# Gelu by ScalarE's own function, a 512-column u pass, half as many compressed-score products, and norm weights folded into w_out, in a one-core hybrid decoder block

## The chip, the cores and the metric

The kernel runs on one core of a Trainium2 chip. The metric is the device time of one execution in microseconds (us). A profile of one execution lies beside it: what each engine did and what it waited for. The engines are TensorE (PE; its weight loads are listed apart as PEld), VectorE (DVE), ScalarE (ACT), GpSimd (POOL) and SyncE (SP), which issues all the transfers.

## The reference, cut to what matters

One layer of a decoder block on 512 tokens of width 1024. One input projection gives u and v (512 columns each), q (512), the keys and values (768) and 24 gate logits. Group A is a spatial gate: gelu(u) times a causal mix of layer_norm(gelu(v)). Group B is sparse attention with three branches; the compressed branch scores each query against 31 compressed keys:

```
a = spatial_gating_unit(gelu(u), gelu(v), ...)
s_cmp = einsum('bthgd,bnhd->bhgtn', q, kc) * scale
p_cmp = masked_softmax(s_cmp, cmp_end[None, :] <= t_pos[:, None])
b = gated sum of the compressed, selected and window branches
mixed = concatenate([rms_norm(a, mix_out_g[0]), rms_norm(b, mix_out_g[1])])
x = x + mixed @ w_out
x = x + memory_cross_attention(rms_norm(x), mem, ...)
x = x + square(relu(rms_norm(x) @ w_ff1)) @ w_ff2
```

gelu is the tanh form, 0.5 z (1 + tanh(0.798 (z + 0.0447 z^3))).

## The kernel before, in words

Every float32 operand of a product is split in two: a rounded high part (`hi`) and the rest (`lo`). `mm3` makes one product of three: hi by hi, hi by lo, lo by hi. A weight block comes in by `granule`: one transfer into `raw`, then `hi` as a copy (on ACT or DVE, whichever the planner finds sooner) and `lo` as a subtraction on DVE.

The program text doesn't issue anything by itself. It records operations in a `Plan`, and `Plan.schedule` sets the order: it walks through time with a cost for each operation, and among the operations that could start first on an engine it takes the one with the highest rank. The rank is the operation's place in the text, moved by the number that the table `LEADS` holds for its stage (`u0`, `ln`, `pc13`, `wo_b1`, ...). The engines then run their instructions strictly in that order. All instructions therefore bear the line of `issue` (L393 to L397), and groups are told apart by tiles: `ps` is a PSUM bank, `w` and `raw` weight blocks, `b` a large buffer, `z`, `q` and `P` work tiles of 512 columns.

The stages that the change touches:

- The v and u projections (`proj`), recorded as fill work beside the attention: v as one pass of 512 columns, u as two passes of 256 (`u0`, `u256`). ACT moves each result out of PSUM with the scale `rx`. Then `gelu2` makes gelu of two ACT functions (Square, Tanh) and two DVE operations per tile of 512 columns, and gives 2 gelu(z); the norms after it put the factor right with 4 EPS.
- `cprep`, once for each of 4 token blocks and 2 key heads: for each of 4 heads one product of the queries `qT` (128 columns of weights) with the high and one with the low part of the compressed keys `KC`, 32 columns each, into one bank on top of the mask `cmk` (a product with the identity). DVE takes the maximum and subtracts it, ACT takes Exp, DVE sums, divides and gates, and PE transposes the tile `pc`.
- `evac`, which collects the attention's output in `bT`; for a finished token block it takes the mean square and multiplies `bT` by the norm weights `gmx[:, 1]` on DVE. `wo_b` splits `bT` and multiplies with the second half of w_out.

The attention's scores, softmax (Exp on ACT, tile `P`), scaling (DVE or POOL), transposes and value products run through all of this.

Of the kernel before, what the change touches and what calls it, by code (L numbers as in the profile page):

```python
# [10 lines left out]
F32R = mybir.dt.float32r  # L11
# [44 lines left out]

LEADS = {"ch_f0": -786, "ch_f1": -935, "ch_norm0": -3881, "ch_norm1": -4239, "ch_norm3": -5516, "ch_o0": 272,
# [20 lines left out]


class Plan:  # L80
# [14 lines left out]
    WARM = 6400  # L95

    SPARE = (0, 300, 0, 0, 0)

    def __init__(self, tc, share):
        self.tc, self.nc, self.share = tc, tc.nc, share  # L100
        self.ops, self.loads, self.lead, self.queue, self.stage, self.stages = [], [], 0.0, None, None, []
        self.home, self.last, self.reads = {}, {}, {}
        self.tiles, self.uses, self.caps, self.index = [], [], {}, {}
        for e in self.ENGINES:
            setattr(self, e, self._Engine(self, e))
# [31 lines left out]
    def cost(self, eng, op, aps, func):  # L137
# [5 lines left out]
        if eng == "sync":  # L143
            run = min(list(a.ap)[-1][1] for a, _ in aps)
            return max(450, 4 * n * max(list(a.ap)[0][1] for a, _ in aps) / (260 if run <= 128 else 360))
        psum = any(bank for _, bank in aps)
# [15 lines left out]
    def locks(self, eng, op, reads, writes):  # L162

        if eng == "gpsimd":
            return op not in ("memset", "affine_select")
        if eng != "vector":
            return False
        inner = [a for a in reads if self.width(a) > 1 and not self.in_bank(a)]
        if op == "square":
            return len(inner) == 1  # L170
        if op in ("tensor_copy", "tensor_scalar"):
            return self.width(writes[0]) > 16 and len(inner) == 1
        return op in ("tensor_tensor", "scalar_tensor_tensor") and len(inner) > 1
# [27 lines left out]
    def add(self, ways, args, kw):  # L201
# [7 lines left out]
        for group, write in ((reads, False), (writes, True)):  # L209
            for a in group:  # L210
# [41 lines left out]
                for e, op in ways]  # L252
        self.loads.append(self.load(ways[0][1], args[1]) if ways[0][0] == 0 else 0.0)
        self.stages.append(self.stage)
        self.ops.append((ways, args, kw, sorted(deps), used, self.lead + LEADS.get(self.stage, 0) - i))

    def schedule(self):
# [13 lines left out]
        ends = [{} for _ in self.tiles]  # L271
        free, begun = [0.0] * ne, 0.0

# [26 lines left out]
        def start(i, e):  # L300
            t = max(free[e], begun + self.loads[i]) if e == 0 else free[e]
            if e in port and next(w for w in ops[i][0] if w[0] == e)[3]:
                t = max(t, port[4 - e])
            for x in range(ne):
                t = max(t, known[i][x] + lat[x][e])
            return t
# [31 lines left out]
        while len(out) < len(ops):  # L338
# [26 lines left out]
            if e == 0:  # L365
                begun = t
            span = max(span, end)
            if shared:
# [32 lines left out]
def hybrid_block(ctx, tc, x, mem, norm_mix_g, w_in, sg_ln_g, sg_ln_b, sg_w, sg_b, q_norm_g,  # L401
# [92 lines left out]

    def granule(src, keep=False, before=None):

# [13 lines left out]
        if before:  # L510
            for i in range(a):
                before(i)
                c = slice(i * b, i * b + b)
                dma(raw[:, c], src[:, i, :])
                split_any(raw[:, c], hi[:, c], lo[:, c])
        else:
            dma(raw.rearrange("p (a b) -> p a b", a=a), src)
            split_any(raw, hi, lo)
        hi, lo = (v.rearrange("p (a b) -> p a b", a=a) for v in (hi, lo))
        return [(hi[:, i, :], lo[:, i, :]) for i in range(a)]  # L520

    def grans(w, k0, nk, c0, ncol):
        v = w.rearrange("(k p) n -> p k n", p=P)
        step = min(nk, 1024 // ncol)
        r = []
        stage = nc.stage
        for k in range(k0, k0 + nk, step):
            nc.stage = f"{stage}.w{c0}.{k}"
            r += granule(v[:, k:k + step, c0:c0 + ncol])
        nc.stage = stage  # L530
        return r
# [124 lines left out]
    VBv = VB.rearrange("p (b h t) d -> p b h t d", b=2, h=NKV)  # L656
    KC = cpool.tile([P, 2, NKV, 32], F32R, name="KC")
    gates = cpool.tile([P, TT, 24], F32, name="gates")
# [193 lines left out]
    for i in range(2):  # L852
        nc.tensor.transpose(tp[:, i * HD:i * HD + HD].bitcast(F32R), kch[:, i].rearrange("p s d -> p (s d)"),
                            idr[:HD, :HD])
    nc.scalar.copy(KC, tp.rearrange("p (i h n) -> p i h n", i=2, h=NKV))

# [9 lines left out]
    vz = b8([P, TT, SG], F32)  # L866
    ps = proj(512, 512)
    for t in range(TT):
        act(vz[:, t, :], ps[t], AF.Copy, scale=rx[:, t:t + 1])
    nc.stage = "ln"  # L870
    gelu2([(vz[:, t, :], ztile()) for t in range(TT)])
    mvs, rvs = [], []
    for t in range(TT):
# [3 lines left out]
        mvs.append(mv)  # L877
        rvs.append(rsqrt(mv[:, 1:2], 1.0, 4.0 * EPS))
    for t in range(TT):
# [3 lines left out]
        split(w, vbh[:, t, :], vbl[:, t, :])  # L883
    for c in (0, 256):
        nc.stage = f"u{c}"
        ps = proj(c, 256)
        nc.stage = f"gu{c}"
        for t in range(TT):
            act(u2[:, t, c:c + 256], ps[t][:, :256], AF.Copy, scale=rx[:, t:t + 1])
        gelu2([(u2[:, t:t + 2, c:c + 256], ztile().rearrange("p (t c) -> p t c", t=2)) for t in (0, 2)])  # L890

# [24 lines left out]
    def cprep(t, kvh, qT):  # L916

        ps = bank()[:, :G * 32].rearrange("p (g n) -> p g n", g=G)
        nc.tensor.matmul(ps, idb, bc(cmk[:, t, None, :], [P, G, 32]), start=True, stop=False)
        for g in range(G):  # L920
            for i in range(2):
                nc.tensor.matmul(ps[:, g, :], qT[:, g * P:g * P + P], KC[:, i, kvh, :], start=False,
                                 stop=g == G - 1 and i == 1)
        mx, den, c = small(G), small(G), small(G)
        dve.tensor_reduce(mx, ps, AX.X, OP.max)
        e = zpool.tile([P, G, 32], F32, tag="pc", bufs=2, name=nm("pc"))
        dve.tensor_tensor(e, ps, bc(mx[:, :, None], [P, G, 32]), OP.subtract)
        act(e, e, AF.Exp)
        dve.tensor_reduce(den, e, AX.X, OP.add)
        dve.reciprocal(c, den)  # L930
        g3 = gates[:, t, :].rearrange("p (h b) -> p h b", b=3)
        dve.tensor_tensor(c, c, g3[:, kvh * G:kvh * G + G, 0], OP.mult)
# [8 lines left out]
    class Pair:  # L941
# [79 lines left out]
        def evac(self):  # L1021
# [12 lines left out]
            if kb == 3:  # L1034
# [3 lines left out]
                rb[t] = rsqrt(stats(ps, SG), 1.0 / SG, EPS)  # L1038
                dve.tensor_tensor(bT[t], bT[t], bc(gmx[:, 1, :, None], [P, 4, P]), OP.mult)

# [76 lines left out]
    for t in range(TT):  # L1117
        ra.append(rsqrt(stats(u2[:, t, :], SG), 1.0 / SG, 4.0 * EPS))

# [64 lines left out]
    def wo_b(t):  # L1184
        if not wso:
            wso.extend(p for blk in range(2) for p in grans(w_out2, 4, 4, blk * 512, 512))
        bh, bl = qpair()
# [238 lines left out]
```

## Time and profile before

| | us |
|---|---|
| median of 3 runs | 705.9 |
| the 3 runs | 703.88, 707.63, 705.9 |
| the profiled execution, its time | 703.69 |
| its span, first to last instruction | 701.8 |

The span is what the trace shows; 1.9 us of the profiled execution's time lie outside it. Busy time of an engine is the time in which at least one of its instructions ran; a product's own duration is longer than the distance to the next one, since products overlap, so costs of products are read from start to start.

### The profile page before, as it was taken

How to read it: one execution, taken by the hardware profiler on the slowest of the kernel's cores; microseconds unless marked ns; L12 is line 12 of the kernel's file. 1: busy time of each engine (PE TensorE's matmuls, PEld its weight loads, DVE VectorE, ACT ScalarE, POOL GpSimd, SP SyncE). 2: the span in 40 equal slices, each digit the busy share in tenths (PEclk: the TensorE clock that was granted, in tenths of full speed). 3: DMA queues.
4: the chain of work that ended last, by engine and by line, in shares of the span. 5: the costliest groups of instructions: out<-in, count | busy, mean ns of one | idle time of the engine just before them, and what ended most of it. 6: DMA issues, size and time to landing. Idle time of an engine off the chain costs nothing.

```text
span 701.8 us, 9905 instructions
## 1 busy us (share of the span) xinstructions
PE 694.0 (99%) x3768; PEld 588.2 (84%) x3768; DVE 424.4 (60%) x794; ACT 316.6 (45%) x643; POOL 78.8 (11%) x118
## 2 busy tenths in 40 slices
PE   8999999999999999999999999999999999999997
PEld 7898879988888889889888888888888888888886
DVE  6596899998899898679844223332225344433433
ACT  6454467877778776476434124332123122111210
POOL 1002112141330421133000000000000000000000
PEclk9999999999999999999999999999999999999999
DMA  9633543445222000414143332333213322223203
GB/s 291 173 101 98 189 126 122 146 136 163 61 91 98 24 1 1 150 32 120 32 118 93 96 111 83 99 99 111 91 61 121 116 94 90 91 101 109 91 0 121
DMA packets 64702, 71.05 MB, mean 101 GB/s; under 512 B 3160, under 2 KB 48976, under 8 KB 64656
## 3 DMA queue, kind: packets, MB, share of 16 engines
q1 hardware_dynamic: 64656, 70.42, 32.2%
q8 instruction: 30, 0.49, 0.3%
q14 instruction: 16, 0.13, 0.1%
HBM read 68.32 MB, written 2.10 MB: 100 GB/s over the span
## 4 chain that ended last, share of the span: by engine, by line
PE 94%; DMA 2%; DVE 2%; ACT 1%; issue 1%; SPq 0%; DVEq 0%; ACTq 0%
PE ps L397 94%; DMA raw<-in_w_in_dram 1%; DVE w L397 1%; DMA raw<-in_cmp_w_dram 1%; DMA b<-in_x_dram 1%; DVE b L397 1%; DVE z L397 0%; ACT w L397 0%; ACT b L397 0%; DVE s L397 0%; SPq L397 0%; ACT z L397 0%; ACT q L397 0%; DVEq L1421 0%; ACTq L397 0%
## 5 line engine op out<-in xcount | busy, mean ns | idle before, releaser
L397 PE MATMUL ps<-w,q 128*128 128x512 f32 x960 | 225.4, 391 | 0.0
L397 PEld LDWEIGHTS ps<-w,q 128*128 128x128 f32 x960 | 178.5, 188 | 36.0
L397 ACT CAST w<-raw 128x1024 fp32r<-128x1024 f32 (+2 forms) x95 | 97.8, 1034 | 237.4 <-PE ps L397 221.4
L397 DVE TENSOR_TENSOR w<-raw,w 128x1024 fp32r<-128x1024 f32 (+2 forms) x117 | 137.8, 1181 | 96.9 <-ACT w L397 96.2
L397 PE MATMUL ps<-w,b 128*128 128x512 f32 (+3 forms) x928 | 187.0, 355 | 1.1 <-DVE w L397 0.8
L397 PEld LDWEIGHTS ps<-w,b 128*128 128x128 f32 (+1 forms) x928 | 149.4, 187 | 24.3 <-DVE w L397 1.9
L397 PE MATMUL ps<-b,w 128*128 128x512 f32 x720 | 164.6, 389 | 0.0
L397 PEld LDWEIGHTS ps<-b,w 128*128 128x128 f32 x720 | 134.8, 188 | 27.7
L397 DVE TENSOR_TENSOR b<-ps,b 128x512 fp32r<-128x512 f32 (+2 forms) x88 | 54.3, 635 | 12.4 <-ACT b L397 8.9
L397 PE MATMUL ps<-b,b 128*128 128x256 f32 (+1 forms) x344 | 57.3, 294 | 0.0
L397 ACT CAST b<-ps 128x512 fp32r<-128x512 f32 (+1 forms) x84 | 44.5, 551 | 21.3 <-PE ps L397 20.4
L397 DVE CAST q<-b 128x512 fp32r<-128x512 f32 x24 | 10.3, 427 | 70.2 <-PE ps L397 70.2
L397 PEld LDWEIGHTS ps<-b,b 128*128 128x128 f32 x344 | 48.2, 192 | 1.5 <-ACT b L397 0.4
L397 POOL TENSOR_SCALAR P<-P,s,gates 128x128 f32<-128x128 f32 (+3 forms) x53 | 33.5, 643 | 92.9 <-DVE s L397 58.7
L397 PE MATMUL ps<-idf,P 128*128 128x128 f32 x192 | 38.3, 280 | 0.0
L397 ACT ACTIVATE P<-ps,s 128x128 f32<-128x128 f32 (+3 forms) x64 | 33.7, 533 | 7.0 <-DVE s L397 6.7
L397 DVE TENSOR_REDUCE s<-ps 128x2 f32<-128x512 f32 (+4 forms) x64 | 35.3, 564 | 2.5 <-PE ps L397 2.1
L397 ACT ACTIVATE z<-ps 128x512 f32<-128x512 f32 (+3 forms) x43 | 23.0, 581 | 27.7 <-PE ps L397 27.7
L397 DVE CAST w<-raw 128x1024 fp32r<-128x1024 f32 (+2 forms) x22 | 13.8, 631 | 31.3 <-PE ps L397 30.6
L397 POOL TENSOR_TENSOR r<-s,negh 128x1 f32<-128x1 f32 (+2 forms) x25 | 20.3, 815 | 98.0 <-DVE s L397 97.9
L397 PE MATMUL ps<-b,q 128*128 128x256 f32 (+2 forms) x96 | 27.5, 347 | 0.5 <-ACT q L397 0.5
L397 PEld LDWEIGHTS ps<-idf,P 128*128 128x128 f32 x192 | 24.2, 141 | 1.2 <-POOL P L397 0.4
(156 smaller groups left out, 576.7 us busy)
## 6 DMA issues: line engine op xcount, KB each, us to landing
raw<-in_w_ff_dram SPq DMA_DIRECT2D x64, 512.0 KB, 4.0
raw<-in_w_in_dram SPq DMA_DIRECT2D x12, 512.0 KB, 3.9
raw<-in_cmp_w_dram SPq DMA_DIRECT2D x8, 512.0 KB, 4.2
raw<-in_w_out_dram SPq DMA_DIRECT2D x8, 512.0 KB, 3.9
raw<-in_w_mkv_dram SPq DMA_DIRECT2D x8, 512.0 KB, 3.8
b<-in_x_dram SPq DMA_DIRECT2D x8, 256.0 KB, 4.9
raw<-in_w_in_dram SPq DMA_DIRECT2D x8, 256.0 KB, 5.2
b<-in_x_dram SPq DMA_DIRECT2D x4, 512.0 KB, 4.2
```

The lines of the kernel that those rows point to most:

```text
L397: getattr(getattr(self.nc, eng), op)(*a, **k)
```

## The change

`gelu2` stays for the small compression network alone. For u and v ACT now applies `Gelu_apprx_tanh` while it moves the result out of PSUM: one instruction per tile, with the same scale. It gives gelu itself, so the norms use EPS. The planner learns that this function and Exp/Tanh belong to different tables and that a change of table costs ACT a load (1283 in `TABLE`). u is projected in one pass of 512 columns. `KC` holds high and low part of a head side by side, so `cprep` makes one product of 64 columns per head; DVE adds mask and halves. The multiplication of `bT` by the norm weights goes; the second half of w_out is split with a scale instead (`gain`). The planner's transfer costs, its rule on when GpSimd holds the port that it shares, and the whole table `LEADS` are new, so every engine's order is new.

```
-LEADS = {"ch_f0": -786, "ch_f1": -935, ...
+LEADS = {"ch_f0": -1174, "ch_f1": -1572, ...
...
+    TABLES, TABLE = {AF.Exp: 0, AF.Tanh: 0, AF.Gelu_apprx_tanh: 1}, 1283
...
-            return max(450, 4 * n * max(list(a.ap)[0][1] for a, _ in aps) / (260 if run <= 128 else 360))
+            return max(450, 4 * n * max(list(a.ap)[0][1] for a, _ in aps) / (230 if run <= 128 else 290))
...
-            return op not in ("memset", "affine_select")
+            return op != "dma_start"
...
+            if e == 2 and self.tables[i] not in (None, table):
+                t += self.TABLE
...
-            split_any(raw, hi, lo)
+            for i in range(a if gain is not None else 0):
+                c = slice(i * b, i * b + b)
+                split(raw[:, c], hi[:, c], lo[:, c], scale=gain[:, i:i + 1])
+            if gain is None:
+                split_any(raw, hi, lo)
...
-    KC = cpool.tile([P, 2, NKV, 32], F32R, name="KC")
+    KC = cpool.tile([P, NKV, 2, 32], F32R, name="KC")
...
-        act(vz[:, t, :], ps[t], AF.Copy, scale=rx[:, t:t + 1])
+        act(vz[:, t, :], ps[t], AF.Gelu_apprx_tanh, scale=rx[:, t:t + 1])
     nc.stage = "ln"
-    gelu2([(vz[:, t, :], ztile()) for t in range(TT)])
...
-    for c in (0, 256):
-        nc.stage = f"u{c}"
-        ps = proj(c, 256)
-        nc.stage = f"gu{c}"
-        for t in range(TT):
-            act(u2[:, t, c:c + 256], ps[t][:, :256], AF.Copy, scale=rx[:, t:t + 1])
-        gelu2([(u2[:, t:t + 2, c:c + 256], ztile().rearrange("p (t c) -> p t c", t=2)) for t in (0, 2)])
+    nc.stage = "u"
+    ps = proj(0, SG)
+    nc.stage = "gu"
+    for t in range(TT):
+        act(u2[:, t, :], ps[t], AF.Gelu_apprx_tanh, scale=rx[:, t:t + 1])
...
-        nc.tensor.matmul(ps, idb, bc(cmk[:, t, None, :], [P, G, 32]), start=True, stop=False)
         for g in range(G):
-            for i in range(2):
-                nc.tensor.matmul(ps[:, g, :], qT[:, g * P:g * P + P], KC[:, i, kvh, :], start=False,
-                                 stop=g == G - 1 and i == 1)
+            nc.tensor.matmul(ps[:, g], qT[:, g * P:g * P + P], KC[:, kvh], start=True, stop=True)
...
-        dve.tensor_reduce(mx, ps, AX.X, OP.max)
-        dve.tensor_tensor(e, ps, bc(mx[:, :, None], [P, G, 32]), OP.subtract)
+        dve.tensor_tensor(e, ps[:, :, 1, :], bc(cmk[:, t, None, :], [P, G, 32]), OP.add)
+        dve.tensor_tensor(e, ps[:, :, 0, :], e, OP.add)
+        dve.tensor_reduce(mx, e, AX.X, OP.max)
+        dve.tensor_tensor(e, e, bc(mx[:, :, None], [P, G, 32]), OP.subtract)
...
-                dve.tensor_tensor(bT[t], bT[t], bc(gmx[:, 1, :, None], [P, 4, P]), OP.mult)
...
-            wso.extend(p for blk in range(2) for p in grans(w_out2, 4, 4, blk * 512, 512))
+            wso.extend(p for blk in range(2) for p in grans(w_out2, 4, 4, blk * 512, 512, gain=gmx[:, 1]))
```

The order of PE before, at the first compressed scores (`ps_303`): mask, then eight products with `KC`, among the attention's first scores (`KL`, `tri`) and the first u pass (`w_275`).

```order
L397 MATMUL ps_298<-b_9_89,q_290 128x256
L397 LDWEIGHTS idb
L397 MATMUL ps_303<-cmk,idb 128x128
L397 MATMUL ps_303<-KC,q_290 128x32 x8
L397 MATMUL ps_298<-KL,q_290 128x256
```

The same scores (`ps_291`) in the changed kernel: their four products stand in turn with transposes of the mixing matrix `wg`, behind products of the u pass of 512 columns (`ps_266`, `ps_267`). The first of them:

```order
L405 MATMUL ps_266<-w_275,b_8_86 128x512
L405 MATMUL ps_266<-w_277,b_6_84 128x512
L405 MATMUL ps_267<-w_275,b_6_84 128x512
L405 MATMUL ps_291<-KC,q_278 128x64
L405 MATMUL ps_689<-idf,wg 128x128
```

The scores' tile `pc_295` comes back to PE as a transpose; the four rows ahead of it and itself:

```order
L405 MATMUL ps_267<-w_277,b_6_84 128x512 x2
L405 MATMUL ps_267<-w_277,b_8_86 128x512
L405 MATMUL ps_267<-w_277,b_6_84 128x512 x2
L405 MATMUL ps_267<-w_277,b_8_86 128x512
L405 MATMUL ps_296<-idf,pc_295 128x128
```

From the last product with `KC` to this transpose stand one transpose of `wg` and 40 products of 512 columns of the u pass, and nothing else. The mask's product is gone, and there are four products with `KC` where eight stood.

The order of ACT before, at the end of v's gelu: Square and Tanh of `b_139` through the tiles `z`, then the attention's first Exps (`P`), with no load of a table.

```order
L397 ACTIVATE b_139_233<-ps_237,rx 128x512
L397 CAST q_290<-ps_291 128x512
L397 ACTIVATE z_249<-b_139_233 128x512
L397 ACTIVATE z_248<-z_248 128x512
L397 CAST w_287<-raw_286 128x1024
L397 ACTIVATE z_249<-z_249 128x512
L397 ACTIVATE P_295,s_294<-ps_292,s_293 128x128
L397 ACTIVATE P_296,s_294<-ps_292,s_293 128x128
```

The same place in the changed kernel, from the copy of `KC` that PE's four products wait for to the Exp of `pc_295`: two loads of a table stand in the queue, one ahead of three Gelus (v's third and fourth tile, u's first), one ahead of the Exps.

```order
L405 CAST KC<-ps_228 128x2x2x32
L405 CAST b_136_230<-z_262 128x512
L405 ACT_TABLE_LOAD
L405 ACTIVATE b_139_233<-ps_236,rx 128x512
L405 ACTIVATE b_139_233<-ps_237,rx 128x512
L405 ACTIVATE b_138_232<-ps_266,rx 128x512
L405 CAST b_136_230<-z_263 128x512
L405 ACT_TABLE_LOAD
L405 ACTIVATE P_289,s_288<-ps_286,s_287 128x128
L405 ACTIVATE P_290,s_288<-ps_286,s_287 128x128
L405 ACTIVATE pc_295<-pc_295 128x128
```

Over the whole program ACT has one load of a table before and seven after: three times to Gelu's table and back, all around the v and u passes.

## Rows read from the trace of the kernel before

**Rows 1.** The page, busy time by engine: us, share of span, instructions.
```profile
PE 694.0 (99%) x3768; PEld 588.2 (84%) x3768; DVE 424.4 (60%) x794; ACT 316.6 (45%) x643; POOL 78.8 (11%) x118
```

**Rows 2.** Chain of work that ended last, in order of time: start, us, what.
```profile
81.26 5.79 DMA raw<-in_w_in_dram
...
95.41 34.39 PE ps L397 x267
...
133.06 88.46 PE ps L397 x557
...
221.65 476.44 PE ps L397 x2401
```

**Rows 3.** Waits of PE over the whole span: us in total, times, longest.
```profile
PE ps L397 <- DVE zero L397: 1.1, 1, 1.1
PE ps L397 <- DMA b<-in_x_dram: 0.9, 1, 0.9
PE ps L397 <- DVE w L397: 0.8, 1, 0.8
PE ps L397 <- ACT q L397: 0.5, 1, 0.5
PE ps L397 <- DVE z L397: 0.4, 1, 0.4
```

**Rows 4.** Timeline of PE around the first compressed scores: start, us, instructions merged.
```profile
110.36 0.23 PE L397 MATMUL ps<-cmk,idb 128*128 128x128 bf16 x1
110.40 1.04 PE L397 MATMUL ps<-KC,q 128*128 128x32 f32 x8
111.30 0.36 PE L397 MATMUL ps<-KL,q 128*128 128x256 f32 x1
...
111.54 17.52 PE L397 MATMUL ps<-w,b 128*128 128x256 f32 x144
128.90 0.88 PE L397 MATMUL ps<-b,b 128*128 128x256 f32 x6
```

**Rows 5.** Timeline of PE in the second feed-forward product, a long unbroken run.
```profile
525.17 155.00 PE L397 MATMUL ps<-w,q 128*128 128x512 f32 x683
```

**Rows 6.** Busy time in one window: PE, PEld, DVE, ACT, POOL; clock, DMA share, GB/s.
```profile
100.00:140.00 40.00, 39.47 (x318) 37.84 (x317) 38.21 (x81) 32.46 (x83) 7.32 (x13) 1.00 0.36 120
```

**Rows 7.** Groups of ACT's instructions by shape: busy us, mean ns | idle before.
```profile
L397 ACT ACTIVATE b<-ps,rx 128x512 f32<-128x512 f32 x12 | 8.0, 685 | 7.9 <-PE ps L397 7.9
...
L397 ACT ACTIVATE P<-ps,s 128x128 f32<-128x128 f32 x16 | 5.8, 364 | 4.2 <-DVE s L397 4.1
...
L397 ACT ACTIVATE z<-b 128x512 f32<-128x512 f32 x8 | 5.1, 634 | 0.1
L397 ACT ACTIVATE z<-z 128x512 f32<-128x512 f32 x8 | 5.0, 628 | 0.7 <-DVE z L397 0.7
L397 ACT ACTIVATE b<-ps,rx 128x256 f32<-128x256 f32 x8 | 3.6, 477 | 1.6 <-PE ps L397 1.6
...
L397 ACT ACTIVATE pc<-pc 128x128 f32<-128x128 f32 x8 | 2.5, 316 | 1.8 <-DVE pc L397 1.7
...
L397 ACT ACT_TABLE_LOAD x1 | 1.3, 1283 | 0.8 <-PEq L1412 0.8
```

**Rows 8.** Groups of DVE's instructions by shape, the same columns.
```profile
L397 DVE TENSOR_TENSOR w<-raw,w 128x1024 fp32r<-128x1024 f32 x106 | 129.6, 1225 | 91.9 <-ACT w L397 91.3
...
L397 DVE SCALAR_TENSOR_TENSOR b<-z,b 128x512 f32<-128x512 f32 x8 | 5.5, 689 | 0.4 <-ACT z L397 0.3
...
L397 DVE SCALAR_TENSOR_TENSOR z<-z,b 128x512 f32<-128x512 f32 x8 | 5.5, 688 | 0.6 <-ACT z L397 0.5
...
L397 DVE SCALAR_TENSOR_TENSOR b<-ps,cols,b 128x512 fp32r<-128x512 f32 x4 | 3.0, 748 | 0.1
...
L397 DVE TENSOR_TENSOR bT<-bT,cols 128x512 f32<-128x512 f32 x4 | 2.7, 684 | 0.0
...
L397 DVE TENSOR_TENSOR pc<-ps,s 128x128 f32<-128x128 f32 x8 | 2.3, 286 | 0.1
```

More of the change, by code (lines that the diff above doesn't have):

```diff
@@ L55 @@
          "wf": dict(w=1, raw=1)}
-LEADS = {"ch_f0": -786, "ch_f1": -935, "ch_norm0": -3881, "ch_norm1": -4239, "ch_norm3": -5516, "ch_o0": 272,
[20 rows of a table removed]
+LEADS = {"ch_f0": -1174, "ch_f1": -1572, "ch_f2": -903, "ch_norm1": 1885, "ch_norm2": 867, "ch_norm3": -7928,
[21 rows of a table added]
 class Plan:
@@ L101, in __init__ @@
         self.ops, self.loads, self.lead, self.queue, self.stage, self.stages = [], [], 0.0, None, None, []
-        self.home, self.last, self.reads = {}, {}, {}
+        self.home, self.last, self.reads, self.tables = {}, {}, {}, []
         self.tiles, self.uses, self.caps, self.index = [], [], {}, {}
@@ L253, in add @@
         self.loads.append(self.load(ways[0][1], args[1]) if ways[0][0] == 0 else 0.0)
+        self.tables.append(next((self.TABLES[a] for a in args if isinstance(a, AF) and a in self.TABLES), None))
         self.stages.append(self.stage)
@@ L271, in schedule @@
         ends = [{} for _ in self.tiles]
-        free, begun = [0.0] * ne, 0.0
+        free, begun, table = [0.0] * ne, 0.0, 0
         port = {1: 0.0, 3: 0.0}
@@ L366, in schedule @@
                 begun = t
+            if e == 2 and self.tables[i] is not None:
+                table = self.tables[i]
             span = max(span, end)
@@ L493, in rsqrt, with granule @@
         return r
-    def granule(src, keep=False, before=None):
+    def granule(src, keep=False, before=None, gain=None):
         a, b = src.shape[1:]
@@ L517, in granule, with grans @@
             dma(raw.rearrange("p (a b) -> p a b", a=a), src)
-            split_any(raw, hi, lo)
+            for i in range(a if gain is not None else 0):
[3 more added lines that the diff above has]
+                split_any(raw, hi, lo)
         hi, lo = (v.rearrange("p (a b) -> p a b", a=a) for v in (hi, lo))
         return [(hi[:, i, :], lo[:, i, :]) for i in range(a)]
-    def grans(w, k0, nk, c0, ncol):
+    def grans(w, k0, nk, c0, ncol, gain=None):
         v = w.rearrange("(k p) n -> p k n", p=P)
@@ L528, in grans @@
             nc.stage = f"{stage}.w{c0}.{k}"
-            r += granule(v[:, k:k + step, c0:c0 + ncol])
+            r += granule(v[:, k:k + step, c0:c0 + ncol], gain=gain if gain is None else gain[:, k - k0:k - k0 + step])
         nc.stage = stage
@@ L854, in hybrid_block @@
                             idr[:HD, :HD])
-    nc.scalar.copy(KC, tp.rearrange("p (i h n) -> p i h n", i=2, h=NKV))
+    nc.scalar.copy(KC.rearrange("p h i n -> p i h n"), tp.rearrange("p (i h n) -> p i h n", i=2, h=NKV))
     nc.queue, wqueue[0], nc.stage = "fill", "wf", "v"
@@ L867, in hybrid_block @@
     ps = proj(512, 512)
+    nc.stage = "gv"
     for t in range(TT):
-        act(vz[:, t, :], ps[t], AF.Copy, scale=rx[:, t:t + 1])
+        act(vz[:, t, :], ps[t], AF.Gelu_apprx_tanh, scale=rx[:, t:t + 1])
     nc.stage = "ln"
-    gelu2([(vz[:, t, :], ztile()) for t in range(TT)])
     mvs, rvs = [], []
@@ L877, in hybrid_block @@
         mvs.append(mv)
-        rvs.append(rsqrt(mv[:, 1:2], 1.0, 4.0 * EPS))
+        rvs.append(rsqrt(mv[:, 1:2], 1.0, EPS))
     for t in range(TT):
@@ L916, in cprep @@
     def cprep(t, kvh, qT):
-        ps = bank()[:, :G * 32].rearrange("p (g n) -> p g n", g=G)
-        nc.tensor.matmul(ps, idb, bc(cmk[:, t, None, :], [P, G, 32]), start=True, stop=False)
+        ps = bank()[:, :2 * G * 32].rearrange("p (g i n) -> p g i n", g=G, i=2)
         for g in range(G):
-            for i in range(2):
-                nc.tensor.matmul(ps[:, g, :], qT[:, g * P:g * P + P], KC[:, i, kvh, :], start=False,
-                                 stop=g == G - 1 and i == 1)
+            nc.tensor.matmul(ps[:, g], qT[:, g * P:g * P + P], KC[:, kvh], start=True, stop=True)
         mx, den, c = small(G), small(G), small(G)
-        dve.tensor_reduce(mx, ps, AX.X, OP.max)
         e = zpool.tile([P, G, 32], F32, tag="pc", bufs=2, name=nm("pc"))
-        dve.tensor_tensor(e, ps, bc(mx[:, :, None], [P, G, 32]), OP.subtract)
+        dve.tensor_tensor(e, ps[:, :, 1, :], bc(cmk[:, t, None, :], [P, G, 32]), OP.add)
+        dve.tensor_tensor(e, ps[:, :, 0, :], e, OP.add)
+        dve.tensor_reduce(mx, e, AX.X, OP.max)
+        dve.tensor_tensor(e, e, bc(mx[:, :, None], [P, G, 32]), OP.subtract)
         act(e, e, AF.Exp)
         dve.tensor_reduce(den, e, AX.X, OP.add)
+        g3 = gates[:, t, :].rearrange("p (h b) -> p h b", b=3)
         dve.reciprocal(c, den)
-        g3 = gates[:, t, :].rearrange("p (h b) -> p h b", b=3)
         dve.tensor_tensor(c, c, g3[:, kvh * G:kvh * G + G, 0], OP.mult)
@@ L1117, in hybrid_block @@
     for t in range(TT):
-        ra.append(rsqrt(stats(u2[:, t, :], SG), 1.0 / SG, 4.0 * EPS))
+        ra.append(rsqrt(stats(u2[:, t, :], SG), 1.0 / SG, EPS))
     nc.lead, nc.stage = 1000, "outa"
```

41 rows, old and new, of the table LEADS are left out of this document.

## The prediction

> **What bounds the kernel now.** I read the busy time of the page first: PE works 694.0 of 701.8 us [rows 1]. Then the chain that ended last: from 95.4 us to the end it is PE's own products, but for one detour of 3.3 us that ends at 133.06 [rows 2]; ahead of 95 us it runs for a while over transfers and weight splits, such as the 5.79 us of an input weight. Then PE's waits: after its start (1.1 for the first operand, 0.9 for x) they are 0.8, 0.5 and 0.4 us, 1.7 in all [rows 3]. So the time is the length of PE's stream. Work that other engines save gives at most these 1.7 us; a product taken out of PE's stream gives its whole distance; and an engine that becomes late can cost without any such bound. Busy time doesn't tell the distance between products, since they overlap: that has to be read from starts.
>
> **The change part by part.**
>
> *u in one pass.* The run of 256-column products that starts at 111.54 and holds 144 of them is followed at 128.90: 17.36 us / 144 = 0.1206 us each [rows 4]. Products of 512 columns follow each other at 155.0 / 683 = 0.227 us [rows 5]. u takes 8 blocks of its inner dimension x 4 token blocks x 3 products: before 2 x 96 = 192 of 256 columns, 192 x 0.1206 = 23.2 us; after 96 of 512, 96 x 0.227 = 21.8 us. Gain 1.4 us. It is small because a 256-column product costs little more than half of a 512-column one. The other side of the bound: if the 512-column products ran as those of the 256-column run per column, 96 x 0.241, the gain would be nothing.
>
> *Compressed scores.* Eight products of 32 columns start at 110.40 and the next instruction at 111.30: 0.90 / 8 = 0.1125 us each, nearly as long as a product of 256 columns (0.1206) in the same rows [rows 4]. So what they cost is not their columns, and 64 columns lie between two widths with almost one price: I take 0.1125 (0.1206 at most). 64 products become 32: 32 x 0.1125 = 3.6 us (3.3 at 0.1206). The mask's product goes 8 times; from its start to the next is 0.04 us [rows 4], so 0.3 us. Where the new products stand in turn with transposes the distance may be another; I found no reason for a sign.
>
> PE's stream is shorter by 1.4 + 3.6 + 0.3 = 5.3 us.
>
> *Gelu.* DVE loses 16 operations of 0.69 us on 512 columns, 11.0 us [rows 8]. ACT loses 8 Squares of 0.634 and 8 Tanhs of 0.628, 10.1 us, and 8 evacuations of 0.477 become 4 of 0.685, 1.1 us [rows 7]. I take a Gelu to last as long as the scaled evacuation that it replaces, 0.685: the Tanh of the same width (0.628) is no longer than the Square (0.634), so the function does not seem to matter. Against that stand six loads of a table; the one load of the trace took 1.283 us [rows 7], 7.7 us for six. ACT comes out 3.5 us shorter. These things happen about 100 to 140 us, where DVE is busy 38.2 of 40 us and ACT 32.5, so that ACT had 7.5 us to spare there [rows 6]. None of it is on PE's path by itself; the gain is bounded by the waits, 1.7 us, and the harm by what the loads hold up.
>
> *What the loads hold up.* ACT's queue is in order, so everything behind a load waits. I worked it through for the tightest loop that the order shows, the second pair of loads. From the copy of KC on, ACT has two copies and three Gelus of at most 0.685 (3.4), two loads (2.6), two Exps of 0.364 and the Exp of pc, 0.316 [rows 7]: 7.0 us. DVE then sums, divides, gates and scales: four operations of at most 0.286 [rows 8], 1.1 us, so pc is ready some 8.2 us after the copy. PE goes in that time through the four products with KC and four transposes (8 x some 0.11, 0.9 us) and 40 products of 0.227 (9.1 us): 10.0 us before it asks for pc. That leaves 1.8 us, or 0.9 us for each load beyond its 1.283. So I cost the loads at nothing; their cover is the u pass itself, which stands as 40 products ahead of the transpose. If the cover went, the whole 7.7 us would be in the open.
>
> The Trainium skill says more of this: ScalarE: Activation LUTs, What ACT_TABLE_LOAD costs, gives about 1283 ns for the load and about 1380 ns for a drain, 2.66 us for every switch, and its rules advise batching by table set, which three round trips do not. The load of this trace agrees with 1283; no instruction here stands close enough behind it to show the drain. By the page's figure this pair would take 2.8 us more, 1.0 beyond the slack, and an estimate over the three pairs is at most 3 us, a time of 703.6.
>
> *Scores on DVE.* cprep gets two more operations on 128 columns, 8 x 2 x 0.286 = 4.6 us [rows 8], spread over the whole attention. DVE's total gain stays: 11.0 - 4.6 = 6.4. Behind the extra 0.57 us per call stands the Exp of pc; the slack above still covers it, since ACT comes to that Exp 6.7 us after the copy.
>
> *Norm weights.* Four multiplications of bT of 0.684 leave DVE [rows 8]. Four splits of 1.225 on DVE become eight of 0.748, 1.1 us more, so DVE gains 1.6 us; ACT takes eight scaled copies of at most 0.685, 5.5 us, for four that either engine made. All of it is preparation of weights that PE uses after fill work. I take nothing, between -0.5 and +1 us.
>
> *The new order.* The transfers, the table of leads and the planner's costs change every queue. u's four transfers hold the same bytes in half as many rows. The places with waits before, ahead of 95 us, hang on transfers [rows 2]; the order can remove 1.7 us or add as much. I take nothing.
>
> **Sum.** The profiled execution took 703.69 us, near the low end of the runs shown; 703.7 - 5.3 = 698.4. On the median of 705.9 that is 700.6, and that is the forecast: **700.5 us**.
>
> **Rivals.**
> 1. *The relief counts too.* DVE is at 96% in the window of 100 to 140 us [rows 6] and loses 11 us there; the waits of 1.7 us go as well, and the short detour of the chain at 130 us. 700.6 - 1.7 = 698.9, with the low side of the unknowns some 697. Against it: only 0.5 us of the waits is in that window.
> 2. *Part of it is eaten.* A new order opens waits elsewhere, for a transfer or a late split, of 2 to 9 us, or the loads are as long as the page says: 702.5 to 709. PE is so full that any engine's lateness shows, which speaks for it; that ACT and DVE have less to do speaks against.
> 3. *Slower.* The six loads stand in the open: each holds up the Exps behind it, the tiles P come late, their transposes stop PE, and since the attention hands work on from pair to pair nothing is won back. At 1.283 us that is 7.7 - 5.3 = +2.4, 708.3, still within half a per cent. It becomes slower than that bound when each load costs more than (5.3 + 3.5) / 6 = 1.47 us in the open. At twice the row's 1.283 it gives 15.4 - 5.3 = +10.1, 716. For it: the queue is in order and Exps do stand behind each load. Against it: the slack of 1.8 us counted above.
> 4. *The shorter products don't get shorter in sum*: a 64-column product costs twice a 32-column one. Then only 1.4 + 0.3 is left, 704.2. The rows for 32 and 256 columns speak against it; I count it within rival 2.
>
> **How the numbers follow.** Half a per cent, 3.5 us, is about what a measurement of this kernel tells from no change, so faster means under 702.4 and slower over 709.4. The forecast alone, 698.9 to 702.4: 0.53. Rival 1: 0.14. Rivals 2 and 4: 0.21. Rival 3 beyond its point: 0.12. Faster 0.67, same 0.21, slower 0.12. The range leaves out rival 3 and the end of rival 2, and below reaches under rival 1 by the 2 us in which the runs shown differ from their median: 694.5 to 706.
>
> **What would show it.** Right: the runs of u at 96 products of 0.227; products with KC at about 0.11 from start to start, 32 of them; PE's busy time near 689; six loads between 95 and 140 us, each near 1.28, and no wait of PE on P, pc, q or b of over 1 us there; DVE's busy share in that window far down. Wrong: PE idle in the window of the loads, released by ACT; gaps on ACT behind each load; waits on w or raw in the first 100 us that are longer than before; or a span over 704 with PE's waits unchanged, which would mean that the distances between products in the new order are longer than those read here.

## The result and the profile after

The changed kernel takes 699.98 us (median of 5 runs) against 705.58 for the kernel before in the same comparison: a ratio of 0.9926, interval 0.9901 to 0.9952. That is 5.6 us less, faster by 0.7%; forecast were 700.5. The profiled execution took 699.56 us, with a span of 697.8; that is 4.0 us less than the span of 701.8 before, whose execution was near the low end of its runs.

The busy line of the page after, to be read against [rows 1]:

```profile
PE 689.5 (99%) x3632; PEld 579.0 (83%) x3632; DVE 415.2 (59%) x791; ACT 318.2 (46%) x634; POOL 79.2 (11%) x120
```

PE's busy time fell by 4.5 us. DVE lost 9.2 us (the prediction's terms make 11.0 - 4.6 + 1.6 = 8.0), and ACT gained 1.6 (-3.5 for the Gelus and loads, up to +5.5 for the scaled splits): near what was counted.

PE's waits after, for [rows 3]:

```profile
PE ps L405 <- DMA b<-in_x_dram: 1.1, 1, 1.1
PE ps L405 <- DVE zero L405: 1.1, 1, 1.1
PE ps L405 <- ACT z L405: 0.7, 1, 0.7
PE ps L405 <- DVE w L405: 0.7, 2, 0.5
PE ps L405 <- DVE b L405: 0.4, 1, 0.4
PE ps L405 <- ACT q L405: 0.2, 1, 0.2
```

Behind the two of the start, the small waits are 2.0 us. Before they were 1.9: to the 1.7 of [rows 3] comes one that it doesn't show:

```profile
PE ps L397 <- ACT w L397: 0.2, 1, 0.2
```

New are 0.7 us for ACT's `z` at 521 us and 0.4 for DVE's `b` at 135 us; those of DVE's `z` and of ACT's `w` went, that of ACT's `q` shrank. So the gain did not come from waits; the stream itself is shorter.

PE around the first compressed scores, for [rows 4]: start, us, instructions merged.

```profile
102.23 7.54 PE L405 MATMUL ps<-w,b 128*128 128x512 f32 x32
109.70 0.25 PE L405 MATMUL ps<-idr,z 64*128 64x64 f32 x1
...
111.58 0.19 PE L405 MATMUL ps<-KC,q 128*128 128x64 f32 x1
111.61 0.30 PE L405 MATMUL ps<-idf,wg 128*128 128x128 f32 x1
111.67 0.28 PE L405 MATMUL ps<-KC,q 128*128 128x64 f32 x1
...
112.26 9.38 PE L405 MATMUL ps<-w,b 128*128 128x512 f32 x40
121.47 0.27 PE L405 MATMUL ps<-idf,pc 128*128 128x128 f32 x1
```

Four products with `KC` and four transposes go from 111.58 to 112.26, 0.68 us in turn. The u products follow each other at 9.21 / 40 = 0.230 us here and 7.47 / 32 = 0.233 in the run at 102 us, which holds some products of v too; both are a little above the 0.227 of [rows 5]. And `pc` is multiplied at 121.47 without a wait.

The same place on ACT, from the copy of `KC` to the Exp of `pc`:

```profile
110.65 0.27 ACT L405 CAST KC<-ps 128x128 fp32r<-128x128 f32 x1
...
111.45 1.28 ACT L405 ACT_TABLE_LOAD   x1
112.75 1.84 ACT L405 ACTIVATE b<-ps,rx 128x512 f32<-128x512 f32 x3
...
115.11 1.28 ACT L405 ACT_TABLE_LOAD   x1
116.41 0.37 ACT L405 ACTIVATE P<-ps,s 128x128 f32<-128x128 f32 x1
...
117.45 0.31 ACT L405 ACTIVATE pc<-pc 128x128 f32<-128x128 f32 x1 [0.24 <-DVE pc L405]
```

From the copy's start to the end of that Exp pass 7.1 us, close to the 7.0 worked out. The instruction behind a load begins 1.30 us after the load's start, 0.02 us after its end. And on DVE, what follows the Exp:

```profile
118.06 0.28 DVE L405 TENSOR_REDUCE s<-pc 128x4 f32<-128x128 f32 x1
118.37 0.23 DVE L405 RECIPROCAL s<-s 128x4 f32<-128x4 f32 x2
118.52 0.73 DVE L405 SCALAR_TENSOR_TENSOR z<-b,s,lngb 128x512 f32<-128x512 f32 x1
119.17 0.16 DVE L405 TENSOR_TENSOR s<-s,gates 128x4 f32<-128x4 f32 x1
120.35 0.69 DVE L405 TENSOR_TENSOR b<-ps,b 128x512 fp32r<-128x512 f32 x1 [1.02 <-ACT b L405]
120.96 0.28 DVE L405 TENSOR_TENSOR pc<-pc,s 128x128 f32<-128x128 f32 x1
```

This part was reckoned at 1.1 us and takes 3.5, from the Exp's end at 117.76 to 121.24: the four operations stand in DVE's queue among others, and one of these waits 1.02 us for ACT. `pc` is ready 0.2 us before PE asks for it; the slack of 1.8 us was not there. That 0.2 us were left is due to PE: it came to its four products 0.93 us after the copy's start (111.58 and 110.65), where the prediction let it start at once.

The window of [rows 6], 100 to 140 us:

```profile
100.00:140.00 40.00, 39.61 (x226) 33.40 (x226) 35.29 (x88) 34.23 (x79) 10.09 (x16) 1.00 0.46 147
```

DVE is busy 35.3 of 40 us where it was 38.2, ACT 34.2 where it was 32.5. And the chain that ended last, some of its pieces, for [rows 2]:

```profile
91.25 41.50 PE ps L405 x230
132.78 2.33 DVE b L405 x5
135.15 81.28 PE ps L405 x507
```

It is PE's stream as before, with a detour at 133 us in both, over DVE and ACT before and over DVE alone after. It takes another one, over short ACT and DVE pieces between 216 and 242 us.

### The profile page after: what moved, and what is told of

It is laid out like the page before. It is cut to its first block, busy times and chain, and to the rows that moved or that the text cites. A ratio compares the mean times of both kernels' runs of the same rounds, so it can differ in the third digit from the quotient of the medians.

```text
span 697.8 us, 9634 instructions
## 1 busy us (share of the span) xinstructions
PE 689.5 (99%) x3632; PEld 579.0 (83%) x3632; DVE 415.2 (59%) x791; ACT 318.2 (46%) x634; POOL 79.2 (11%) x120
## 4 chain that ended last, share of the span: by engine, by line
PE 92%; DVE 3%; ACT 3%; DMA 1%; issue 0%; SPq 0%; DVEq 0%; ACTq 0%
PE ps L405 92%; DVE b L405 1%; DVE w L405 1%; ACT w L405 1%; ACT b L405 1%; DMA raw<-in_cmp_w_dram 1%; ACT P L405 1%; DMA raw<-in_w_in_dram 1%; DVE s L405 0%; ACT KL L405 0%; DVE pc L405 0%; ACT z L405 0%; DVE P L405 0%; SPq L405 0%; DVE q L405 0%
## 5 line engine op out<-in xcount | busy, mean ns | idle before, releaser
L405 DVE TENSOR_TENSOR w<-raw,w 128x1024 fp32r<-128x1024 f32 (+2 forms) x113 | 133.0, 1178 | 113.0 <-ACT w L405 112.4
L405 PEld LDWEIGHTS ps<-w,b 128*128 128x128 f32 (+1 forms) x832 | 142.9, 186 | 27.4 <-DVE w L405 2.7
L405 PE MATMUL ps<-b,b 128*128 128x256 f32 x344 | 58.7, 293 | 0.0
L405 ACT CAST b<-ps 128x512 fp32r<-128x512 f32 (+1 forms) x84 | 44.0, 552 | 17.6 <-PE ps L405 16.9
L405 POOL TENSOR_SCALAR P<-P,s,gates 128x128 f32<-128x128 f32 (+3 forms) x55 | 35.4, 653 | 90.2 <-DVE s L405 76.9
L405 PE MATMUL ps<-idf,P 128*128 128x128 f32 x192 | 34.9, 281 | 0.0
L405 DVE TENSOR_REDUCE s<-ps 128x2 f32<-128x512 f32 (+3 forms) x56 | 32.5, 602 | 0.3 <-PE ps L405 0.2
L405 DVE TENSOR_TENSOR q<-b,q 128x512 fp32r<-128x512 f32 (+1 forms) x36 | 23.7, 657 | 4.6 <-ACT q L405 3.7
L405 PE MATMUL ps<-b,q 128*128 128x256 f32 (+2 forms) x96 | 26.0, 339 | 0.2 <-ACT q L405 0.2
```

Of the source, the lines that this page charges most:

```text
L405: getattr(getattr(self.nc, eng), op)(*a, **k)
```

## The experiments

Each is the changed kernel with one edit, unless said otherwise. Times are medians, ratios are to the kernel before. The changed kernel itself has a ratio of 0.9926 above and 0.9923 as a yardstick below; 0.001 of ratio is 0.7 us.

**The yardstick.** No edit.

> The changed kernel itself once more, beside the other kernels of this call: the yardstick. Ratio to the kernel before 0.992 to 0.993. The first 12 us hang on when the first transfers land and differ by up to 2 us between executions; from there to the end the trace should agree with the first one within 0.5 us.

Measured: 700.01 us, ratio 0.9923 (0.9904 to 0.9941). Its span differs from the other's by 0.7 us, all of it in the wait for x at 6 us.

**Products of 32 columns again.**

```
+ elif eng == "tensor" and op == "matmul" and self.stages[i][:2] == "pc":
+     for h in range(2):
+         self.nc.tensor.matmul(a[0][:, h, :], a[1], a[2][:, h, :], **k)
```

> The changed kernel in its own order, but each 64-column product of the compressed scores is issued as two of 32 columns, high part and low part. Forecast's reason (a product this narrow costs its fixed 0.1125 us whatever its columns): 32 more products, +3.6 us over the changed kernel's span of 697.8, about 701.4, PE busy about 693. Rival (a 64-column product costs twice a 32-column one, so that halving their number saved nothing): +0, 697.8. Rival (the new order made the gain, the parts did not): within 1 us of 697.8.

Measured: 704.14 us, ratio 0.9973 (0.9961 to 0.9986), 0.0047 to 0.0050 above the changed kernel: 3.3 to 3.5 us, give or take 2. PE's timeline:

```profile
112.72 0.29 PE L406 MATMUL ps<-KC,q 128*128 128x32 f32 x2
112.86 0.33 PE L408 MATMUL ps<-idf,wg 128*128 128x128 f32 x1
...
113.87 1.40 PE L408 MATMUL ps<-w,b 128*128 128x512 f32 x5
```

From the first product to the run behind them pass 1.15 us instead of 0.68: 0.47 / 4 = 0.118 us for each product added, 3.8 us for 32. Rival 4, a product of 64 columns as dear as two of 32, is out.

**u in 256-column products.** All but the first and last product of each bank are issued as two halves.

```
+ elif (eng == "tensor" and op == "matmul" and self.stages[i][:2] == "u."
+       and not k["start"] and not k["stop"]):
+     for h in (0, 256):
+         self.nc.tensor.matmul(a[0][:, h:h + 256], a[1], a[2][:, h:h + 256], **k)
```

> The changed kernel in its own order, but 88 of the 96 products of the u pass (all but the first and the last of each bank) are issued as two of 256 columns. Forecast's reason: 88 x (2 x 0.1206 - 0.227) = +1.25 us, span 699.0. If the 512-column products of this stretch follow each other at 0.230 as in the changed kernel's own rows: 88 x 0.0112 = +1.0. Rival (one pass saved nothing, the order did it): +0.

Measured: 701.87 us, ratio 0.9946 (0.9929 to 0.9962), 1.4 to 1.6 us above, give or take 2: by the medians alone it may be nothing. The distances decide:

```profile
104.52 4.00 PE L406 MATMUL ps<-w,b 128*128 128x256 f32 x32
108.36 0.87 PE L408 MATMUL ps<-w,b 128*128 128x512 f32 x3
```

3.84 / 32 = 0.120 us each, so 96 x (2 x 0.120 - 0.231) = 0.9 us. The two traces agree: from the last unsplit products ahead (at 99.75 us in the changed kernel, 101.00 here) to the transposes of `b` (135.15 and 137.36) the stretch is 0.96 us longer; another 1.25 us were lost ahead of it, where nothing was edited.

**No loads.** Tanh in place of Gelu for u and v, the order unchanged.

```
+ elif len(a) > 2 and a[2] is AF.Gelu_apprx_tanh:
+     self.nc.scalar.activation(a[0], a[1], AF.Tanh, **k)
```

> The changed kernel in its own order, but Tanh stands where Gelu stood, so u and v get another function and ACT loads one table instead of seven. Forecast's reason (the six loads are covered by the u pass): 0 to -0.5 us, the 0.4 us wait of PE at 135 us going at most; span 697.3 to 697.8. Rival (the loads are in the open): -7.7 us, 690. Between them (part of the loads is on the path): -1 to -4.

Measured: 700.75 us, ratio 0.9923 (0.9908 to 0.9937). Six loads less are worth nothing, give or take 1.7 us: they were covered, with whatever they bring along.

**Three loads for each one.** At each change of table ACT also loads the other one and back, with an operation on one column after each.

```
+ if self.tables[i] != self.now:
+     for f in ((AF.Gelu_apprx_tanh, AF.Exp) if self.tables[i] else (AF.Exp, AF.Gelu_apprx_tanh)):
+         self.nc.scalar.activation(self.scr, self.negh[:, :1], f)
...
```

> The changed kernel in its own order, but at each of the six changes of table ACT goes to the new table, back and to it again, so 12 more loads of 1.283 us, each with a one-column function of some 0.2 us: 18 us more in ACT's queue, 6 us at each pair of loads. Forecast's count of the slack (1.8 us per pair): 6 - 1.8 = 4.2 us late at each of three pairs, about +12, 710. The changed kernel's trace shows pc ready only 0.2 us ahead of PE's transpose: if that is all the slack, about +17, 715. If nothing of ACT here is on PE's path: +0 to +2.

Measured: 719.43 us, ratio 1.0189 (1.0173 to 1.0205), some 18.7 us above the changed kernel. ACT's queue got 12 x (1.28 + 0.20) = 17.8 us longer. ACT at one change, and PE's longest waits:

```profile
108.88 1.28 ACT L403 ACT_TABLE_LOAD   x1
110.17 0.20 ACT L403 ACTIVATE scr<-negh 128x1 f32<-128x1 f32 x1
110.39 1.28 ACT L403 ACT_TABLE_LOAD   x1
```
```profile
PE ps L411 <- DVE pc L411: 4.9, 1, 4.9
PE ps L411 <- DVE s L411: 3.4, 1, 3.4
PE ps L411 <- ACT b L411: 2.6, 1, 2.6
```

The longest wait is for the tile of the loop worked through in the prediction. The loss did not come out of the queue one for one: of the 20.0 us by which the profiled span grew, 12.2 are PE idle, less than was added, and 7.8 are PE busy for longer; in the window of 134 to 138 us, right behind the longest wait, the granted clock is 0.66. The six loads are free, and behind them is little reserve.

**The multiplication of bT again**, on DVE just ahead of each split of `bT`.

```
+ if self.stages[i][:4] == "wo_b" and op in ("copy", "tensor_copy") and a[1].tensor.name[:2] == "bT":
+     v = a[1].rearrange("p (k t) -> p k t", k=4)
+     self.nc.vector.tensor_tensor(v, v, self.gmx[:, 1, :, None].to_broadcast([P, 4, P]), OP.mult)
...
```

> The changed kernel in its own order, but each of the four blocks bT is multiplied by the norm weights on DVE once more, just ahead of its split (so these weights act twice and the output is another). 4 x 0.684 us more on DVE, right ahead of the tiles that the second half of w_out waits for. Forecast's reason (covered by fill work): 0 to +0.5 us. Rival (the last block's split is on PE's path after the attention): +0.7 for one block to +2.7 for all four.

Measured: 703.07 us, ratio 0.9957 (0.9942 to 0.9972), 2.4 us above the yardstick, give or take 1.7. The last token block's transposes show part of it, PE's timeline:

```profile
272.95 0.33 PE L408 MATMUL ps<-idf,bT 128*128 128x128 f32 x1 [0.79 <-DVE bT L401]
```

In the changed kernel no wait stands there. PE's wait for the split of an input weight at 91 us is 1.1 us longer too (1.6 for 0.5), ahead of the edit. So the work was not free where I put it back. But here the multiplication stands ahead of these transposes; in the kernel before a block's transposes come first (for the last block the last of them at 274.9 us and the multiplication at 275.3), and PE has no wait for `bT`. So the 0.8 us come from the new place, and this run doesn't tell what the work cost at its old one.

**Empty tables of leads**, the changed kernel and the kernel before, each in the order that the planner finds by its costs alone.

```
-LEADS = {"ch_f0": ...
+LEADS = {}
```

> The changed kernel with an empty table LEADS, so that the planner's order is untuned. To be read against the kernel before with an empty table. Forecast's reason (PE's stream is 5.3 us shorter whatever the order): 5 us less than that one, 2 to 8 with what the orders differ by; PE busy less by 4 to 5.5. Rival (the new table made the gain): no difference, or the other sign. If the planner alone leaves the six loads uncovered: more than that one by up to 3.

> The kernel before with an empty table LEADS: the other half of the comparison. Slower than the kernel before, since its order is no longer tuned: I put 3 to 15 us, with longer waits of PE in the trace.

Measured: the changed kernel 725.34 us, ratio 1.0284 (1.0262 to 1.0306); the kernel before 719.75, ratio 1.0208 (1.0182 to 1.0233). Without a fitted order the change costs 5.6 us (give or take 2.4), the other sign than expected, although PE is busy for 700.2 us against 704.4. PE's idle time grew by more, from 16.9 to 23.2 us; the profiled execution of the kernel before was the slowest of its four, so its trace shows only part of the 5.6. The longest wait, in the changed kernel on PE, and what DVE did meanwhile:

```profile
217.38 0.45 PE L384 MATMUL ps<-idf,pc 128*128 128x128 f32 x1 [5.08 <-DVE pc L384]
```
```profile
212.12 0.28 DVE L384 TENSOR_TENSOR pc<-ps,pc 128x128 f32<-128x128 f32 x1
212.32 0.74 DVE L384 SCALAR_TENSOR_TENSOR w<-raw,cols,w 128x512 fp32r<-128x512 f32 x1
212.98 0.28 DVE L384 TENSOR_REDUCE s<-pc 128x4 f32<-128x128 f32 x1
...
216.95 0.28 DVE L384 TENSOR_TENSOR pc<-pc,s 128x128 f32<-128x128 f32 x1
```

The longer chain for `pc` (mask, half, maximum, subtraction, then the four behind Exp) stands on DVE in turn with the new scaled splits of w_out, four of them of 0.74 us between the add of the halves and the last scaling. In the kernel before, without leads too, the longest wait for `pc` is 1.0 us.

**Which part of the change loses in that order?** Empty table with Tanh for Gelu (the edit of the run without loads), and empty table with the planner's former costs:

> The changed kernel with an empty table of leads, as before (725.3 us, ratio 1.028), and with Tanh in place of Gelu for u and v, which needs no load of a table and is another function; the planner still reckons with the loads, so the order of every engine is that of the run with Gelu. Four of its loads go, 5.1 us of ACT's queue. Theory A: the loads are why the untuned order lost 5.6 us against the untuned order of the kernel before (719.7): PE's waits on pc, q and P follow ACT one for one, and the time falls by 5 to 8 us to 717 to 720, a ratio of 1.016 to 1.020. Theory B: the waits come from the other parts of the order (DVE's longer chain for pc, transfers), and the time falls by under 2 us: 723.5 to 725.3.

```
-            return max(450, 4 * n * max(list(a.ap)[0][1] for a, _ in aps) / (230 if run <= 128 else 290))
+            return max(450, 4 * n * max(list(a.ap)[0][1] for a, _ in aps) / (260 if run <= 128 else 360))
...
-            return op != "dma_start"
+            return op not in ("memset", "affine_select")
```

> The changed kernel with an empty table of leads, and the planner's costs for transfers (260 and 360 instead of 230 and 290) and its rule on when GpSimd holds the shared port as they were in the kernel before. Theory A (the loads and the computation itself decide): within 3 us of the run with the new costs, 722 to 728, a ratio of 1.024 to 1.032. Theory B (the new costs are what the untuned order lost by): near the untuned kernel before or better by its 4.2 us of shorter stream, 715 to 720, a ratio of 1.014 to 1.021. More than 3 us above 725 would mean that the new costs help and hide a larger loss.

Measured: 725.01 us, ratio 1.0279 (1.0265 to 1.0293), and 724.33, ratio 1.0268 (1.0250 to 1.0287). Neither is apart from 725.34. So neither the four loads nor the planner's costs are the reason; the wait for `pc` is 5.1 us in all three. The DVE chain is left as the likeliest cause, argued from the rows and not tried.

**DVE's work put back.** Three operations of 256 columns on a scratch tile behind each Gelu's place, 24 of 0.426 us, 10.2 us in all.

```
+ if len(a) > 2 and a[2] is AF.Gelu_apprx_tanh:
+     for _ in range(3):
+         self.nc.vector.scalar_tensor_tensor(self.scr, self.scr, 1.0, self.scr, OP.add, OP.mult)
...
```

> The changed kernel with DVE work put back where it was taken away: behind the place of each of the eight Gelus DVE gets three operations on 256 columns of a scratch tile that nothing reads, some 0.41 us each by the rows of that width, 24 x 0.41 = 9.8 us in all, nearly the 11.0 us that the change took from DVE there. ACT and PE do what they did. Theory (the prediction's): PE's stream sets the time and DVE's relief is worth at most the small waits, so the time rises by no more than 1.7 us, from 700.0 to at most 701.7, a ratio of at most 0.995. Rival (from the trace after): the tile pc reached PE only 0.2 us before it was asked for, and it was DVE's queue that it stood in; DVE was busy 35.3 of 40 us from 100 to 140 us, so 9.8 us more do not fit, what is over the 40 us (5 us) comes out at PE's waits on pc, q or b, and PE's halved pace behind each wait adds to it: 705 to 709, a ratio of 1.000 to 1.005. Then the relief of DVE was part of the gain, and the 5.3 us of shorter stream could not have been had without it.

Measured: 708.87 us, ratio 1.0049 (1.0037 to 1.0062), 8.9 us above the yardstick, give or take 1.6. My theory falls by a wide margin: nearly all of DVE's 10.2 us came out. PE's waits are 5 us more, three of them:

```profile
PE ps L405 <- DVE pc L405: 2.9, 1, 2.9
...
PE ps L405 <- DVE b L405: 1.3, 2, 0.9
...
PE ps L405 <- DVE z L405: 0.8, 1, 0.8
```

Of the 7.8 us by which the span grew, 5.4 are PE idle and 2.4 are PE busy for longer. Behind the wait for `pc` the granted clock falls, two windows (PE, PEld, DVE, ACT, POOL; clock; DMA):

```profile
127.20:130.00 2.80, 2.80 (x10) 2.18 (x9) 2.80 (x8) 1.48 (x6) 0.88 (x2) 0.55 0.42 116
130.50:135.00 4.50, 4.50 (x23) 3.77 (x22) 4.36 (x9) 2.78 (x4) 0.00 (x0) 0.96 0.35 127
```

The 15 products of 512 columns behind that wait take 5.1 us, where they took 3.5 in the changed kernel. The order here is the one fitted to the lighter DVE, and the work came in eight blocks of 1.3 us, three of them between 115 and 121 us, ahead of the last scaling of `pc`; what an order fitted to this load would win back is open.

**The scores alone.** The kernel before with its own table, and only `KC` side by side, four products, mask and halves on DVE.

```
-    KC = cpool.tile([P, 2, NKV, 32], F32R, name="KC")
+    KC = cpool.tile([P, NKV, 2, 32], F32R, name="KC")
...
+            nc.tensor.matmul(ps[:, g], qT[:, g * P:g * P + P], KC[:, kvh], start=True, stop=True)
...
+        dve.tensor_tensor(e, ps[:, :, 1, :], bc(cmk[:, t, None, :], [P, G, 32]), OP.add)
+        dve.tensor_tensor(e, ps[:, :, 0, :], e, OP.add)
```

> The kernel before with its own table of leads and costs and one part of the change alone: high and low compressed keys side by side, one product of 64 columns per head, no mask product, mask and halves added on DVE. The planner makes its order anew from this, so some products change places. Theory (the prediction's): 32 products fewer at 0.1125 and 8 masks fewer at 0.04 are 3.9 us less of PE's stream and the 4.6 us more on DVE are covered: 701.5 to 702.5 against 705.6, a ratio of 0.994 to 0.996. Rival: DVE is busy 38.2 of 40 us from 100 to 140 us in the kernel before; the longer chain for pc and the order that no table was fitted to give the 3.9 us back as waits of PE on pc, q and P, 705 to 709, a ratio of 0.999 to 1.005, with PE's busy time nevertheless 3 to 4 us less.

Measured: 734.41 us, ratio 1.0425 (1.0404 to 1.0447), far outside both expectations. PE's longest wait and what it waits for, on DVE:

```profile
124.83 0.58 PE L397 MATMUL ps<-w,b 128*128 128x256 f32 x1 [9.63 <-DVE w L397]
```
```profile
116.68 0.26 DVE L397 TENSOR_TENSOR pc<-ps,cmk 128x128 f32<-128x128 f32 x1
...
123.56 1.21 DVE L397 TENSOR_TENSOR w<-raw,w 128x1024 fp32r<-128x1024 f32 x1
```

The split of u's next weights stands at 123.56 behind some 11 us of gelu, norm and score work, with which DVE was busy almost without a gap. This run can't price the scores, since their code and every engine's order changed together: the table of leads was fitted to another program, and the time is above even that of the kernel before with no table (719.75). PE was busy for 701.4 us, not 3 to 4 us less than before, at a mean granted clock of 0.986. The run does show again that DVE is what runs out around 115 us.

## Why the prediction was right, and where not

*PE's stream sets the time and got shorter by 5.3 us.* Right. The scores (3.6 forecast): 3.3 to 3.5 by undoing them, give or take 2, and 3.8 by the distances. u (1.4): 0.9 by the distances, 1.4 to 1.6 by the medians, give or take 2; the term was sized with the 0.227 of a long run elsewhere, and in this place the distance is 0.231. The mask (0.3) was not tried alone. By distances that is 3.8 + 0.9 + 0.3 = 5.0 of the 5.6 us measured (3.4 to 7.0 by the interval); the two profiled executions show 4.5 us less of PE's busy time. That 700.0 meets 700.5 so closely is in part luck: u came out smaller than forecast and the scores a little larger, and the interval is wider than either difference.

*The loads cost nothing.* Right in time: without them the time is the same. The step behind it was wrong, "That leaves 1.8 us, or 0.9 us for each load": for DVE I added up four durations as if its queue were empty; they took 3.5 us instead of 1.1. ACT's part came out within 0.1 us, in part by luck: its copies and Gelus were shorter than the 0.685 taken, and the sum left out two reads behind the Exps and 0.24 us in which ACT waited for DVE's `pc`. So the longer chain ahead of the Exp was not covered by ACT's queue either. With 3.5 us on DVE the sum would have had PE wait; PE came to its products 0.9 us later than I let it, and 0.2 us of slack were left. Twelve loads more cost 18.7 us. So rival 3's mechanism is real, and was 0.2 us away at this tile. Beside the load, the Trainium skill (ScalarE: Activation LUTs, What ACT_TABLE_LOAD costs) has a drain of some 1380 ns for every switch. The trace does not agree with that: a load takes 1.28 us, and where work stands on both sides of it, it starts 0.02 us after the instruction ahead ends and the next one 0.02 us after its own end.

*Work that other engines save gives at most 1.7 us.* As a bound on the gain it held; the small waits were 1.9 us and even rose to 2.0. The prediction did say that "an engine that becomes late can cost without any such bound", but it priced DVE's relief at its gain only, and did not say that the relief covers the additions. With the relief gone, 8.9 us come out: more than the whole gain. So in this order the shorter stream is had only because DVE got room for it; the 4.6 us of score work lean on the 11.0 us that Gelu took off DVE. That is shown for this order alone: the kernel before has DVE busy 38.2 of 40 us [rows 6] in an order fitted to it, and no wait over 0.6 us there. What the same change without Gelu would take in an order of its own is not shown.

*Norm weights, "I take nothing".* Not settled. Put back just ahead of the split the multiplication costs 2.4 us (0.7 to 4.1), but the 0.8 us that the trace shows as PE's wait come from that place; at its old place PE has no wait for `bT`.

*The new order, "I take nothing".* Right for the two tables as they are, each fitted to its program. It is not a property of the change: without the tables the same change is 5.6 us slower. Rival 2 has waits that a new order opens; that the gain of the whole change could turn into a loss with the order, the prediction did not say, and the rows of before do not show it. How much of the 5.6 us the fitting of the new table itself brought stays open.

*What would show it.* PE's 689.5, the six loads of 1.28 us, no wait over 1 us among them, as written. DVE's share in the window fell by 2.9 us of 40, and not "far down": less work there also let later work move in.

## What to carry to other kernels

When one engine's stream is the time, price a cut in that stream by the distance from start to start, at the place where it is. Then look at the engine next to full, here DVE: its saved work may gain little by itself and still be what the gain stands on, so work out slack through its whole queue, with what stands between the operations that matter and what those wait for. A change and an order fitted to it are one thing; neither can be priced with the other's table.

## What the runs showed of the hardware

A wait of PE can cost more than its length. In the untuned changed kernel PE waits 2.4 us for `P` at 105 us, and again 0.35 us for `KC`; the first 21 of the 512-column products behind them take 7.04 us, where 21 at 0.230 would take some 5. PE's timeline:

```profile
109.34 7.04 PE L384 MATMUL ps<-w,b 128*128 128x512 f32 x21
```

In its first part the granted clock is at 0.50, which is 1.2 of 2.4 GHz, two windows of that kernel:

```profile
109.50:113.00 3.50, 3.50 (x10) 2.73 (x10) 2.93 (x9) 3.47 (x6) 1.09 (x3) 0.50 0.49 150
113.50:116.00 2.50, 2.50 (x13) 2.05 (x12) 2.49 (x10) 1.51 (x3) 0.55 (x1) 0.98 0.00 0
```

The traces of the kernel before and of the changed kernel, which have no wait over 1.1 us, show no such stretch: 1.00 in the windows of 100 to 140 us above and in [rows 6], and a mean over the span of 0.999 and 1.000. The runs with three loads for each one and with DVE's work put back show it too, behind waits of 4.9 and 2.9 us (0.66 and 0.55).
